# Neighbourhood attention's scores with all 128 array rows, band and context in one matmul

## The chip, the cores and the metric

One core of a Trainium2 chip runs the kernel. The metric is device microseconds of one execution; the number compared is the median of several runs. Engines are named TensorE (PE in the profile, PEld its weight loads), VectorE (DVE), ScalarE (ACT), GpSimd (POOL) and SyncE (SP, which issues the transfers).

## What is computed

Two layers of a trunk over 512 latent tokens and 256 context tokens of width 1024. Each layer norms its input, projects it, runs three attention branches (retention, neighbourhood attention, grouped-query attention), gates and merges them. The change concerns neighbourhood attention: 8 heads of 64, each latent query against a band of nearby keys and all 256 context keys, with one softmax over both.

```python
def neighbourhood_attention(q, k, v, kc, vc, rpb, rows):
...
        s = jnp.einsum('brjqhd,brwjkhd->bhrjqwk', qb, kb).astype(jnp.float32) * scale + bias[None]
        s = jnp.where(col_ok[:, :, None, :], s, -jnp.inf)
        s_ctx = jnp.einsum('brjqhd,blhd->bhrjql', qb, kc).astype(jnp.float32) * scale
        s_all = jnp.concatenate([s.reshape(s.shape[:5] + (n_loc,)), s_ctx], axis=-1)
        p = jax.nn.softmax(s_all, axis=-1)
...
        return jnp.einsum('bhrjqwk,brwjkhd->brjqhd', p_loc, vb) + jnp.einsum('bhrjql,blhd->brjqhd', p_ctx, vc)
```

In the first layer the context tokens are queries too: 256 of them attend to the 256 context keys of their head.

## The kernel before

Numbers are carried as two float32r parts, an upper one and the rest, so a product is a sum of matmuls: upper by upper, upper by lower, lower by upper. A projection adds three matmuls for each of 8 feature tiles (L278 to L280: `hxh`, `hxl` are the input's parts, `whi`, `wlo` the weight's) over 512 latent and then 256 context columns. Weights are streamed: SyncE loads `raw`, ScalarE makes `whi` (L262), GpSimd (at times VectorE) makes `wlo` (L264).

In neighbourhood attention one feature tile `p` (0 to 3) holds two heads `e`. For a head, Q (`q`) stands with its upper part in the 64 rows of the head and its lower part in the other 64. `K1` has K's upper part in both halves, so one matmul of 128 rows gives (Q upper + Q lower) by K upper (L588). Q upper by K lower is a second matmul with the 64 rows of the head alone (L589); `K2`, one tile for both heads, has the lower part of head 0 in rows 0 to 63, that of head 1 in rows 64 to 127. In the profile both `K1` and `K2` are called `k`, in the program's order `k1` and `k2`.

A score step `s_step(j)` does this for 128 queries: two matmuls for the band (256 columns from 64 * BAND0[j]), two for the context (256 columns from NX = 512), into one PSUM bank `s` of 512 columns, of which there are two. VectorE adds the bias and takes the maximum (L591), then come the negated maximum (L598), the exponentials on ScalarE (L600), the reciprocal (L602) and the scaling on VectorE or GpSimd (L605). Transposes (L617), their split into parts (L438, L439) and the products with V (L628, L629) follow. The context queries' scores of the first layer go through `smm` (L638, L639), 256 columns a matmul.

TensorE's order is written by hand: `window` lays attention steps and projection matmuls into one stream, by weights and nominal costs that are fixed numbers (0.45 us for a score step). Tile 0 of a layer begins with eight score steps; later the second head's scores go between the first head's transposes and products, and the next tile's between the second's. The other engines' order comes from a scheduler with priorities. `NA.open` takes the memory of the branch, once a layer.

Of the kernel before, what the change touches and what calls it, by code (L numbers as in the profile page):

```python
# [39 lines left out]
def trunk_kernel(ctx: ExitStack, tc: tile.TileContext, xt, wcol, wv, adaw, wbr, wout, nabias, vecs,  # L40
# [26 lines left out]

    # ---------------------------------------------------------------- order of the tensor engine's work
    clock = [0.0]
# [5 lines left out]
    def defer(us, fn):  # L75
        """emit fn once the tensor engine has been given us more microseconds of work"""
        waiting.append([clock[0] + us, len(waiting), fn])
# [69 lines left out]

    # ---------------------------------------------------------------- constants
    npool_cm = pool("nm0")
# [13 lines left out]
    def block_ones(t, blocks):  # L163
        """ones within blocks of partitions, zeros between them"""
        nc.vector.tensor_scalar(t, ident, 0.0, float(len(blocks) == 1), op0=ALU.mult, op1=ALU.add)
        if len(blocks) > 1:
            for a, b in blocks:
                nc.vector.tensor_scalar(t[a:b, a:b], ident[a:b, a:b], 0.0, 1.0, op0=ALU.mult, op1=ALU.add)
        return t
# [30 lines left out]

    # ---------------------------------------------------------------- helpers
    def rsqrt(dst, ss, n, mul, eps):
# [10 lines left out]
    def rsqrt_wide(r, x, t, ss, mul, eps):  # L213
        """r = 1 / sqrt(ss * mul + eps), whole rows of tokens; x and t are scratch"""
        nc.vector.tensor_scalar(x, ss, mul, eps, op0=ALU.mult, op1=ALU.add)
        nc.vector.tensor_scalar(r.bitcast(I32), x.bitcast(I32), -0.5, float(0x5F3759DF), op0=ALU.mult, op1=ALU.add)
        for _ in range(3):
            nc.scalar.activation(t, r, AF.Square)  # L218
            nc.vector.scalar_tensor_tensor(t, t, -0.5, x, op0=ALU.mult, op1=ALU.mult)  # L219
            nc.vector.scalar_tensor_tensor(r, t, 1.5, r, op0=ALU.add, op1=ALU.mult)  # L220

    def col_sums(m, sh, sl, n, tag):
        """sums over the partitions that m groups, on every partition"""
        ss = bank(tag)
        mm(ss[:, :n], lhsT=m, rhs=sh, start=True, stop=False)
        mm(ss[:, :n], lhsT=m, rhs=sl, start=False, stop=True)
        return ss[:, :n]
# [102 lines left out]

    # ---------------------------------------------------------------- modulation
    def ada_load(l, s, apool, bufs):
# [4 lines left out]
    def ada_slice(l, s, apool, bufs, raw=None):  # L337
        """slice s < 8: shift and scale of feature tile s; 8..11: gates of two feature tiles"""
        if raw is None:
# [26 lines left out]

    # ---------------------------------------------------------------- norms
    def sumsq(acc, x, first, c, npool, bufs=2):
# [37 lines left out]

    # ---------------------------------------------------------------- pieces of attention
    def gate_evac(sg):
# [15 lines left out]
    def split_rows(hi, lo, rl, r0, src, scale, cols):  # L424
        rows = slice(r0, r0 + 64)
        nc.scalar.activation(hi[rows, cols], src[rows], AF.Copy, scale=scale)
        nc.vector.scalar_tensor_tensor(lo[rl:rl + 64, cols], src[rows], scale, f(hi[rows, cols]),
                                       op0=ALU.mult, op1=ALU.subtract)
# [13 lines left out]
    def ctx_steps(st, smm, scale, vs, get_ot, r0, ap, bufs):  # L442
        """softmax(s) @ v of the 256 context queries: score, transpose and product steps"""
        def sx():
# [35 lines left out]
        return (0.7, 0.45, sx), (1.0, 0.45, tx), (1.0, 0.45, pvx)  # L480

    def pv_(P, j):
        t, pad = P[j]
        return t[:, :, pad:pad + 256]

    # ---------------------------------------------------------------- neighbourhood attention
    class NA:
# [6 lines left out]
        def open(self):  # L494
            env["gcm"] = pool(f"gp{self.l}")
            env["gp"] = env["gcm"].__enter__()
            self.cm = pool(f"na{self.l}")
            self.ap = self.cm.__enter__()

        def open_work(self):  # L500
# [17 lines left out]
        def u_k(self, p):  # L518
            def ev(ps, o, n):
                if o == 0:  # L520
                    self.K1[p] = [self.ap.tile([128, NT], F32R, tag="k1", name="k1", bufs=4) for _ in range(2)]
                    self.K2[p] = self.ap.tile([128, NT], F32R, tag="k2", name="k2", bufs=2)
                c = slice(o, o + n)
                K1, K2 = self.K1[p], self.K2[p]
                split_rows(K1[0], K2, 0, 0, ps, 1.0, c)
                split_rows(K1[1], K2, 64, 64, ps, 1.0, c)
                nc.vector.tensor_copy(K1[0][64:128, c], f(K1[0][0:64, c]))
                nc.vector.tensor_copy(K1[1][0:64, c], f(K1[1][64:128, c]))
            return u_proj(ap_wcol[self.l][CT_NK + p], G_ALL, ev)
# [28 lines left out]
        def heads(self, p):  # L558
            """score, transpose, product and context steps of the two heads of feature tile p"""
            ap, l = self.wp, self.l  # L560
            heads = []
            for e in range(2):
                r0 = 64 * e
                rr = slice(r0, r0 + 64)
                st = {}
# [12 lines left out]

                def s_step(j, e=e, st=st, rr=rr, start=start):
                    Q, K1, K2 = self.Q[p], self.K1[p], self.K2[p]  # L580
# [4 lines left out]
                    qc = slice(128 * j, 128 * j + 128)  # L585
                    for o, kc in ((0, 64 * BAND0[j]), (256, NX)):
                        kk = slice(kc, kc + 256)
                        mm(s[:, o:o + 256], lhsT=Q[e][:, qc], rhs=K1[e][:, kk], start=True, stop=False)  # L588
                        mm(s[:, o:o + 256], lhsT=Q[e][rr, qc], rhs=K2[rr, kk], start=False, stop=True)  # L589
                    v = BVAR[j]  # L590
# [41 lines left out]

                def smm(s, e=e, rr=rr):
                    Q, K1, K2 = self.Q[p], self.K1[p], self.K2[p]
                    for i in range(2):
                        qc = slice(NX + 128 * i, NX + 128 * i + 128)
                        o = s[:, 256 * i:256 * i + 256]
                        mm(o, lhsT=Q[e][:, qc], rhs=K1[e][:, NX:NT], start=True, stop=False)  # L638
                        mm(o, lhsT=Q[e][rr, qc], rhs=K2[rr, NX:NT], start=False, stop=True)  # L639
                S = [(0.7, 0.45, lambda j=j, s_step=s_step: s_step(j)) for j in range(4)]  # L640
# [7 lines left out]
        def steps(self, p, need):  # L648
            """the second head's scores go beside the first head's products, and the next tile's first head's
            scores (once the projections in need are through) beside the second's"""  # L650
            if p == 0:
# [21 lines left out]

    # ---------------------------------------------------------------- grouped-query attention
    class GQA:
# [26 lines left out]
        def stats_evac(self, t, w, ntok, done, lag):  # L702
            """t = raw * w; sums of squares by token and head, then done(sums)"""
            st = {}
# [208 lines left out]

    # ---------------------------------------------------------------- retention
    class RET:
# [152 lines left out]

    # ---------------------------------------------------------------- merges
    def u_merge(l, b, d, g, m, getpool):  # L1070
# [34 lines left out]

    # ---------------------------------------------------------------- the plan
    plan = []
# [3 lines left out]
    def start_phase(na, first):  # L1111
        """the input norm; the first projections advance feature tile by feature tile"""
        acc = npool.tile([128, NT], F32, name="acc")
# [113 lines left out]

    # weights in the order of use
    def add(us):
# [16 lines left out]
    def finish(l, m, mtp):  # L1246
# [53 lines left out]
        def norm_part(o, n, use, go, w1=3.0, w2=4.0):  # L1300
            """go(wait, fn): run fn, after wait microseconds of other work"""
            r = cp.tile([128, 6], F32, tag="rstd", name="rstd", bufs=2)

            def one():
                ss = stat_mm(accs["t"], o, n)
                nb = n // 128
                rsqrt(r[:, o // 128:o // 128 + nb], ss[:, :nb], nb, 1.0 / D, EPS)
                go(w2, two)

            def two():  # L1310
                bc = bcast_mm(r, o, n)
                for k in range(KT):
                    use(k, bc[:, :n], o, n)
            go(w1, one)
# [48 lines left out]

# [1 line left out]
def _perm():  # L1365
# [111 lines left out]
```

## Time and profile before

| | |
|---|---|
| median of 3 runs | 1785.39 us (1783.95 to 1786.2) |
| span of the profiled execution, first to last instruction | 1782.7 us |
| TensorE busy | 1714.5 us (96%) |
| VectorE busy | 1055.3 us (59%) |
| ScalarE busy | 797.9 us (45%) |
| GpSimd busy | 550.8 us (31%) |
| granted clock of TensorE, mean | 0.995 of full speed |

The span and the runs are 2.7 us apart. The first layer's neighbourhood attention lies at 75.5 to 272 us of the span, the second's at 1058.9 to 1222; the stages with grouped-query attention between about 290 and 560 and between 1240 and 1440. A matmul's row is longer than the time until the next one starts, since matmuls are pipelined: rates are read from the starts of neighbouring rows, not from the durations.

### The profile page before, as it was taken

What the parts mean: (1) busy time and instruction counts of PE and PEld (TensorE: products, weight loads), DVE (VectorE), ACT (ScalarE), POOL (GpSimd) and SP (SyncE); (2) the same over time, 40 slices, a digit from 0 to 9 for tenths busy, and PEclk for the clock granted to TensorE, in tenths of its full rate; (3) what the DMA queues carried; (4) which work ended last, traced back from release to release, by engine and by line L of the source; (5) the groups of instructions that cost most, each with busy time, mean ns of one, the idle gap of its engine ahead of it and who ended that gap; (6) DMA issues with size and microseconds to landing.
All of it is one profiled execution on the core that took longest, in us unless ns stands there. A gap on an engine that the chain in (4) does not pass through costs nothing. (4 is left out here: it accounts for less than half of the span.)

```text
span 1782.7 us, 26397 instructions
## 1 busy us (share of the span) xinstructions
PE 1714.5 (96%) x10068; PEld 1458.9 (82%) x10068; DVE 1055.3 (59%) x2201; ACT 797.9 (45%) x1570; POOL 550.8 (31%) x478
## 2 busy tenths in 40 slices
PE   6999999999999999999999999999999999999997
PEld 4777878888999888888887888777788897887786
DVE  7566467657654565565324755567876645545446
ACT  4355454555553443443223434555555544444342
POOL 1233222333233222222222322332433333333442
PEclk9999999999999999999999999999999999999999
DMA  7211102111111211113536521211111122221245
GB/s 310 74 54 44 55 24 65 43 48 36 48 37 53 65 48 48 60 48 139 217 130 209 170 86 42 78 45 60 60 48 60 48 74 69 69 68 63 90 131 170
DMA packets 43054, 146.40 MB, mean 82 GB/s; under 512 B 4912, under 2 KB 10160, under 8 KB 39856
## 3 DMA queue, kind: packets, MB, share of 16 engines
q1 hardware_dynamic: 42928, 144.72, 24.2%
q8 instruction: 79, 1.29, 0.3%
q14 instruction: 47, 0.39, 0.1%
HBM read 140.51 MB, written 4.19 MB: 81 GB/s over the span
## 5 line engine op out<-in xcount | busy, mean ns | idle before, releaser
L264 POOL TENSOR_TENSOR wlo<-raw,whi 128x512 fp32r<-128x512 f32 x345 | 456.9, 1330 | 975.5 <-ACT whi L262 927.2
L278 PE MATMUL pj<-hxh,whi 128*128 128x512 f32 (+1 forms) x1448 | 531.9, 367 | 10.6 <-DVE ql L967 3.9
L279 PE MATMUL pj<-hxl,whi 128*128 128x512 f32 (+1 forms) x1448 | 509.7, 352 | 0.8 <-DVE hxl L404 0.8
L280 PE MATMUL pj<-hxh,wlo 128*128 128x512 f32 (+1 forms) x1448 | 509.3, 352 | 0.0
L262 ACT CAST whi<-raw 128x512 fp32r<-128x512 f32 x376 | 231.3, 618 | 302.3 <-PE pj L279 220.4
L278 PEld LDWEIGHTS pj<-hxh,whi 128*128 128x128 f32 x1448 | 273.9, 189 | 48.0 <-DVE ql L967 5.8
L280 PEld LDWEIGHTS pj<-hxh,wlo 128*128 128x128 f32 x1448 | 273.6, 189 | 38.9
L279 PEld LDWEIGHTS pj<-hxl,whi 128*128 128x128 f32 x1448 | 274.6, 190 | 26.3 <-DVE hxl L404 1.9
L439 DVE TENSOR_TENSOR pl<-pt,ph 128x512 fp32r<-128x512 f32 (+2 forms) x208 | 127.1, 626 | 63.0 <-ACT ph L438 60.8
L438 ACT CAST ph<-pt 128x512 fp32r<-128x512 f32 (+2 forms) x208 | 108.0, 534 | 91.4 <-PE pt L617 49.5
L278 PE MATMUL pj<-gat,whi 128*128 128x512 f32 (+1 forms) x416 | 144.4, 347 | 2.6 <-ACT gat L910 2.0
L279 PE MATMUL pj<-gat,whi 128*128 128x512 f32 (+1 forms) x416 | 142.4, 342 | 0.5 <-DVE gat L1264 0.3
L280 PE MATMUL pj<-gat,wlo 128*128 128x512 f32 (+1 forms) x416 | 142.1, 342 | 0.0
L310 PE MATMUL pj<-whi,hxh 128*128 128x256 f32 x384 | 111.0, 289 | 1.4 <-DVE kl L967 0.8
L312 PE MATMUL pj<-whi,hxl 128*128 128x256 f32 x384 | 109.3, 285 | 0.0
L311 PE MATMUL pj<-wlo,hxh 128*128 128x256 f32 x384 | 109.3, 285 | 0.0
L278 PEld LDWEIGHTS pj<-gat,whi 128*128 128x128 f32 x416 | 78.8, 189 | 11.9 <-ACT gat L910 2.5
L280 PEld LDWEIGHTS pj<-gat,wlo 128*128 128x128 f32 x416 | 78.8, 190 | 9.3
L855 ACT ACTIVATE p<-p,nm,rq 128x768 f32<-128x768 f32 x64 | 65.4, 1023 | 46.9 <-DVE nm L853 46.4
L279 PEld LDWEIGHTS pj<-gat,whi 128*128 128x128 f32 x416 | 79.0, 190 | 8.9 <-DVE gat L911 0.5
L846 DVE TENSOR_SCALAR_CACHE_REDUCE p<-s 128x384 f32<-128x384 f32 x128 | 69.0, 554 | 26.9 <-PE s L845 25.5
L1099 DVE SCALAR_TENSOR_TENSOR mt<-mt,pj 128x512 f32<-128x512 f32 (+1 forms) x48 | 28.6, 596 | 91.8 <-PE pj L280 91.2
(264 smaller groups left out, 3012.1 us busy)
## 6 DMA issues: line engine op xcount, KB each, us to landing
raw<-in_wcol_dram SPq DMA_DIRECT2D x116, 512.0 KB, 3.5
araw<-in_adaw_dram SPq DMA_DIRECT2D x24, 1024.0 KB, 6.5
raw<-in_wout_dram SPq DMA_DIRECT2D x32, 512.0 KB, 3.5
raw<-in_wbr_dram SPq DMA_DIRECT2D x24, 512.0 KB, 3.5
raw<-in_wv_dram SPq DMA_DIRECT2D x16, 512.0 KB, 3.5
bias<-in_nabias_dram SPq DMA_DIRECT2D x16, 384.0 KB, 3.0
x<-in_xt_dram SPq DMA_DIRECT2D x8, 384.0 KB, 5.7
xo<-in_xt_dram SPq DMA_DIRECT2D x8, 256.0 KB, 3.8
```

The source lines that it names most:

```text
L262: nc.scalar.copy(hi, raw[:, c])
L264: lo_eng.tensor_tensor(lo, raw[:, c], f(hi), op=ALU.subtract)
L278: mm(ps, lhsT=sh, rhs=mh, start=start, stop=False)
L279: mm(ps, lhsT=sh, rhs=ml, start=False, stop=False)
L280: mm(ps, lhsT=sl, rhs=mh, start=False, stop=stop)
L310: mm(o, lhsT=sh[:, tok], rhs=hi, start=(k == 0), stop=False)
L311: mm(o, lhsT=sh[:, tok], rhs=lo, start=False, stop=False)
L312: mm(o, lhsT=sl[:, tok], rhs=hi, start=False, stop=(k == KT - 1))
L438: nc.scalar.copy(ph[:, :n], pt[:, :n])
L439: nc.vector.tensor_tensor(pl[:, :n], pt[:, :n], f(ph[:, :n]), op=ALU.subtract)
L846: nc.vector.tensor_scalar(P[:, jj, kk], s[:, :384], 1.0, -3.0e38, op0=ALU.mult, op1=ALU.max, accum_out=mx[:, i:i + 1])
L855: nc.scalar.activation(P[:, a], P[:, a], AF.Exp, bias=nm[:, a:a + 1], scale=rqe[:, 2 * hf + a:2 * hf + a + 1], accum_out=sm[:, a:a + 1])
```

## The change

K's lower part gets a tile of 128 rows for each head, with zeros in the 64 rows that are not the head's. There are two pairs of such tiles, taken in turn by the feature tiles, as `k2` had two buffers. GpSimd fills the zeros once a layer, when the branch's memory is opened. The second score matmul then uses all 128 rows of Q and of the tile; the lower part of Q meets the zeros. With both operands of full height, band and context go into one matmul of 512 columns, whose moving operand is an access pattern of two blocks of 256 columns, 512 - 64 * BAND0[j] apart (`two_blocks`; for j = 3 the blocks touch). The context queries' scores keep their 256 columns and get the full-height tile. The program also gives its dynamic transfers a smaller scratch. Comments and docstrings that fell away are not shown.

```diff
+    def two_blocks(t, a, b, n):
+
+        v = t[:, a:a + n]
+        return bass.AP(v.tensor, v.offset, [list(v.ap[0]), [b - a, 2], [1, n]])
...
             self.cm = pool(f"na{self.l}")
             self.ap = self.cm.__enter__()
+            self.kz = [[self.ap.tile([128, NT], F32R, name=f"kz{i}{e}") for e in range(2)] for i in range(2)]
+            for pair in self.kz:
+                for e, t in enumerate(pair):
+                    nc.gpsimd.memset(f(t[64 - 64 * e:128 - 64 * e, :]), 0.0)
...
-                    self.K2[p] = self.ap.tile([128, NT], F32R, tag="k2", name="k2", bufs=2)
+                    self.K2[p] = self.kz[p % 2]
...
-                split_rows(K1[0], K2, 0, 0, ps, 1.0, c)
-                split_rows(K1[1], K2, 64, 64, ps, 1.0, c)
+                split_rows(K1[0], K2[0], 0, 0, ps, 1.0, c)
+                split_rows(K1[1], K2[1], 64, 64, ps, 1.0, c)
...
-                    for o, kc in ((0, 64 * BAND0[j]), (256, NX)):
-                        kk = slice(kc, kc + 256)
-                        mm(s[:, o:o + 256], lhsT=Q[e][:, qc], rhs=K1[e][:, kk], start=True, stop=False)
-                        mm(s[:, o:o + 256], lhsT=Q[e][rr, qc], rhs=K2[rr, kk], start=False, stop=True)
+                    kc = 64 * BAND0[j]
+                    mm(s, lhsT=Q[e][:, qc], rhs=two_blocks(K1[e], kc, NX, 256), start=True, stop=False)
+                    mm(s, lhsT=Q[e][:, qc], rhs=two_blocks(K2[e], kc, NX, 256), start=False, stop=True)
...
                         mm(o, lhsT=Q[e][:, qc], rhs=K1[e][:, NX:NT], start=True, stop=False)
-                        mm(o, lhsT=Q[e][rr, qc], rhs=K2[rr, NX:NT], start=False, stop=True)
+                        mm(o, lhsT=Q[e][:, qc], rhs=K2[e][:, NX:NT], start=False, stop=True)
...
-    nc = _bacc.Bacc("TRN2", target_bir_lowering=False, num_devices=1)
+    nc = _bacc.Bacc("TRN2", target_bir_lowering=False, num_devices=1, dynamic_dma_scratch_size=1024)
```

On TensorE the first two score steps of the first layer and the projection behind them read as follows before the change (`s` is the scores' bank, `pj` a projection's):

```order
L588 MATMUL s_805<-k1_579,q_569 128x256
L589 MATMUL s_805<-k2_581,q_569 128x256
L588 MATMUL s_805<-k1_579,q_569 128x256
L589 MATMUL s_805<-k2_581,q_569 128x256
L588 MATMUL s_811<-k1_579,q_569 128x256
L589 MATMUL s_811<-k2_581,q_569 128x256
L588 MATMUL s_811<-k1_579,q_569 128x256
L589 MATMUL s_811<-k2_581,q_569 128x256
L278 MATMUL pj_785<-hxh_171,whi_606 128x512
L279 MATMUL pj_785<-hxl_172,whi_606 128x512
```

Eight matmuls of 256 columns stand ahead of the projection. The same place on TensorE after the change, where L595 and L596 are the two lines of the score step and `kz00` the new tile of head 0:

```order
L595 MATMUL s_812<-k1_587,q_577 128x512
L596 MATMUL s_812<-kz00_566,q_577 128x512
L595 MATMUL s_816<-k1_587,q_577 128x512
L596 MATMUL s_816<-kz00_566,q_577 128x512
L278 MATMUL pj_792<-hxh_171,whi_613 128x512
L279 MATMUL pj_792<-hxl_172,whi_613 128x512
```

Four of 512 columns are left, and nothing else has moved between them and the projection. On GpSimd the start of the first layer before the change reads (`bias` and `pb` are fills for the first two heads):

```order
L264 TENSOR_TENSOR wlo<-raw,whi 128x512 x7
L570 MEMSET bias 128x256
L573 MEMSET pb 128x4x64
L570 MEMSET bias 128x256
L573 MEMSET pb 128x4x64
L264 TENSOR_TENSOR wlo<-raw,whi 128x512 x6
```

The four fills there stand between the seventh and the eighth weight split. The same place on GpSimd after the change, with the zero fills at L507:

```order
L264 TENSOR_TENSOR wlo<-raw,whi 128x512 x7
L507 MEMSET kz_566 64x768
L507 MEMSET kz_567 64x768
L507 MEMSET kz_568 64x768
L264 TENSOR_TENSOR wlo<-raw,whi 128x512
L507 MEMSET kz_569 64x768
L264 TENSOR_TENSOR wlo<-raw,whi 128x512
L578 MEMSET bias 128x256
L581 MEMSET pb 128x4x64
L578 MEMSET bias 128x256
L581 MEMSET pb 128x4x64
L264 TENSOR_TENSOR wlo<-raw,whi 128x512 x4
```

Three zero fills stand ahead of the eighth split, the fourth ahead of the ninth, and the older fills behind it. In the second layer two stand ahead of each of the last two splits before the same place.

## Rows read from the trace of the kernel before

**Rows 1.** Page, part 1: engine, busy us (share of the span), instructions.

```profile
PE 1714.5 (96%) x10068; PEld 1458.9 (82%) x10068; DVE 1055.3 (59%) x2201; ACT 797.9 (45%) x1570; POOL 550.8 (31%) x478
```

**Rows 2.** Stretches: us, busy (count) of PE, PEld, DVE, ACT, POOL; clock, DMA share, GB/s.

```profile
75.50:272.00 196.50, 194.07 (x1089) 155.65 (x1088) 114.03 (x257) 98.35 (x234) 57.73 (x70) 1.00 0.16 50
75.70:89.90 14.20, 14.20 (x54) 9.00 (x53) 7.50 (x25) 5.42 (x14) 3.42 (x6) 1.00 0.29 95
290.00:560.00 270.00, 266.98 (x1691) 239.81 (x1690) 174.69 (x439) 143.14 (x291) 86.12 (x76) 1.00 0.15 45
1058.90:1222.00 163.10, 160.15 (x846) 126.06 (x845) 93.61 (x220) 80.28 (x178) 50.06 (x52) 1.00 0.18 58
1058.90:1073.00 14.10, 14.10 (x52) 8.64 (x50) 6.57 (x22) 6.30 (x15) 4.68 (x5) 1.00 0.24 81
1240.00:1440.00 200.00, 190.56 (x1033) 159.60 (x1032) 143.17 (x370) 110.79 (x212) 74.85 (x58) 1.00 0.18 58
```

**Rows 3.** TensorE's timeline, one score step: start, us, line, out<-in, rows*columns of weights, shapes.

```profile
113.94 0.28 PE L588 MATMUL s<-k,q 128*128 128x256 f32 x1
114.15 0.39 PE L589 MATMUL s<-k,q 64*128 64x256 f32 x1
114.47 0.38 PE L588 MATMUL s<-k,q 128*128 128x256 f32 x1
114.78 0.38 PE L589 MATMUL s<-k,q 64*128 64x256 f32 x1
115.09 0.50 PE L278 MATMUL pj<-hxh,whi 128*128 128x512 f32 x1
115.43 0.39 PE L279 MATMUL pj<-hxl,whi 128*128 128x512 f32 x1
```

**Rows 4.** TensorE's timeline, projections of 256 and 512 columns.

```profile
110.26 0.28 PE L280 MATMUL pj<-hxh,wlo 128*128 128x256 f32 x1
110.38 0.40 PE L278 MATMUL pj<-hxh,whi 128*128 128x512 f32 x1
```

**Rows 5.** Weight loads of the score step in rows 3; idle time before, releaser.

```profile
114.15 0.18 PEld L589 LDWEIGHTS s<-k,q 64*128 64x128 f32 x1 [0.25 <-issue]
```

**Rows 6.** TensorE's timeline, four score matmuls of grouped-query attention, two projections.

```profile
314.78 0.33 PE L844 MATMUL s<-gk,q 128*128 128x384 f32 x1
314.95 0.34 PE L845 MATMUL s<-gk,q 128*128 128x384 f32 x1
315.13 0.34 PE L844 MATMUL s<-gk,q 128*128 128x384 f32 x1
315.31 0.35 PE L845 MATMUL s<-gk,q 128*128 128x384 f32 x1
315.49 0.40 PE L278 MATMUL pj<-hxh,whi 128*128 128x512 f32 x1
315.72 0.40 PE L279 MATMUL pj<-hxl,whi 128*128 128x512 f32 x1
```

**Rows 7.** Lines L589 and L639: count, ns min/median/max, first and last start.

```profile
L589 PE MATMUL s<-k,q x128: 377/381/385, 75.9 to 1203.2; 64*128 64x256 f32 x128
L639 PE MATMUL s<-k,q x16: 377/381/382, 97.2 to 261.4; 64*128 64x256 f32 x16
```

**Rows 8.** TensorE's timeline, first matmul of a context step and the projection behind.

```profile
96.97 0.28 PE L638 MATMUL s<-k,q 128*128 128x256 f32 x1
...
98.12 0.50 PE L278 MATMUL pj<-hxh,whi 128*128 128x512 f32 x1
```

**Rows 9.** ScalarE's timeline, one exponential in the first layer's start.

```profile
79.60 0.72 ACT L600 ACTIVATE pa<-pa,nm 128x512 f32<-128x512 f32 x1 [1.42 <-DVE nm L598]
```

**Rows 10.** GpSimd's timeline, a fill and two weight splits; idle time before, releaser.

```profile
50.36 0.31 POOL L570 MEMSET bias<- 128x256 f32 x1
...
55.53 1.30 POOL L264 TENSOR_TENSOR wlo<-raw,whi 128x512 fp32r<-128x512 f32 x1 [2.72 <-ACT whi L262]
...
1028.15 1.27 POOL L264 TENSOR_TENSOR wlo<-raw,whi 128x512 fp32r<-128x512 f32 x1 [4.11 <-ACT whi L262]
```

More of the change, by code (lines that the diff above doesn't have):

```diff
@@ L563, in heads @@
                 r0 = 64 * e
-                rr = slice(r0, r0 + 64)
                 st = {}
@@ L577, in start, with s_step @@
                         st[nm] = ap.tile([128, 4], F32, tag=nm, name=nm, bufs=2)
-                def s_step(j, e=e, st=st, rr=rr, start=start):
+                def s_step(j, e=e, st=st, start=start):
                     Q, K1, K2 = self.Q[p], self.K1[p], self.K2[p]
@@ L631, in pv_step, with smm @@
                         pv_out(st["ops"], NX, self.get_ot(p), r0, 0)
-                def smm(s, e=e, rr=rr):
+                def smm(s, e=e):
                     Q, K1, K2 = self.Q[p], self.K1[p], self.K2[p]
```

## The prediction

> **What bounds the kernel now.** I read the page's busy times first. TensorE is busy for 1714.5 us, 96% of a span of 1782.7 us [rows 1]. A busy TensorE may still be stalled inside its busy time, so I went on to the two stretches of neighbourhood attention. In the first layer TensorE is idle for 196.50 - 194.07 = 2.4 us of 196.5, in the second for 163.10 - 160.15 = 3.0 us of 163.1 [rows 2]. Nothing that other engines do is on the path there: whatever shortens TensorE's own stream shortens the run, until somebody else is late.
>
> Then the stream itself, by the starts of neighbouring rows. One score step is four matmuls of 256 columns [rows 3]. The reader should see the steps between starts: 0.21, 0.32, 0.31, 0.31 us, so 1.15 us from the first score matmul to the projection behind it, and then 0.34 us until the next projection. An undisturbed 256-column matmul takes 0.12 us between starts [rows 4] and an undisturbed projection of 512 columns 0.23 us (the last two of [rows 6]). So four matmuls that should take 0.48 us take 1.15, and they delay the one behind them by another 0.10. Every second matmul of the step has 64 rows of weights, the others 128. The weight load of the first 64-row matmul stands idle for 0.25 us with "issue" as the releaser, that is, with no semaphore behind it [rows 5]. The grouped-query attention is the counterexample in the same trace: four score matmuls of 384 columns, all with 128 rows, go at 0.17, 0.18, 0.18 and 0.18 us, 0.71 us for half as many columns again, and the projection behind them loses nothing [rows 6]. So the stall sits at each change between 128 and 64 rows, not in the columns.
>
> **The change part by part.** (1) Score steps. There are 128 of the 64-row score matmuls, two to a step, so 64 steps [rows 7]. A step becomes two matmuls of 512 columns with 128 rows. Their price is the projection's 0.23 us each [rows 6], also what the grouped-query rows give per column (0.178 x 512 / 384 = 0.237). So 0.46 us instead of 1.15 + 0.10: 0.79 us less for each, 64 x 0.79 = 50.6 us.
>
> (2) Context steps of the first layer: 16 of the 64-row matmuls, two to a step, 8 steps [rows 7]. One takes 1.15 us now [rows 8] plus the 0.10; afterwards it is four 256-column matmuls of 128 rows, 4 x 0.12 = 0.48. 8 x 0.77 = 6.2 us.
>
> Both lie wholly on the path: 56.8 us. What no row shows is a moving operand of two separate blocks, since every one in these rows is contiguous. I price it like a contiguous one, because the same columns are streamed; a better price than 0.23 us has no row, and a worse one is a rival below. The order of instructions on VectorE, ScalarE and SyncE stays as it was but for rows that change places at three points, and on TensorE the score rows alone differ, so no other wait is added there.
>
> [...]
>
> (3) What comes back as waits. TensorE now runs ahead faster than VectorE and ScalarE were used to. The hard place is the start of each layer's stretch: eight score steps with only a few projections between them. In 14.2 us (first layer) VectorE is busy 7.5 us, and in 14.1 us (second) 6.6 us [rows 2]. TensorE's need there falls by 8 x 0.79 = 6.3 us to 7.9 and 7.8 us. VectorE has to read each score bank before its buffer (there are two) is used again, and its queue holds, behind those reads, reciprocals that wait for ScalarE's exponentials, 0.72 us each and two to a pair [rows 9]. If everything fits, 0 comes back. If VectorE has to sit through two such pairs of about 1.8 us (with their accumulator reads), the stage takes 7.5 + 3.6 = 11.1 us and 3.2 us come back. I take 2.0 for each, since VectorE's need of 6.6 to 7.5 us is close to the 7.9 before any stop for ScalarE.
>
> For the rest of the stretches the nearest rows are the grouped-query stages, which already run full-height scores. There TensorE is idle 3.0 us of 270.0 (1.1%) with VectorE 65% busy, and 9.4 of 200.0 (4.7%) with 72% [rows 2]. After the change the two stretches of together 360 us last some 303, with VectorE at (114.0 + 93.6) / 303 = 69%. In between, about 3%, or 9 us, against 5.4 us now: +3.6 with the starts included. At 1.1% it would be 3.3 us, no increase; at 4.7%, 14.2, an increase of 9. I take +5 in all (two starts at 2.0 and 1.0 elsewhere); the ends are 0 and 9 + 2 x 3.2 = 15.
>
> (4) The zero fills: four per layer, 64 x 768, on GpSimd. The nearest row is 0.31 us for 128 x 256 [rows 10], so 0.93 us each and 3.7 us a layer. In the first layer three take the place of the bias fills from 50.36 us on and are through at about 53.2; the weight split behind them starts at 55.53 today, because it waits for ScalarE's upper part [rows 10]. The fourth pushes the next split back by 0.9 us and the bias fills behind that, which nobody reads before the stretch at 75.7 [rows 2]. In the second layer GpSimd is idle for 4.11 us at the place [rows 10], and one split starts up to 1.9 us later, behind two fills; its reader is the last part of a token projection which has not begun. So the idle time hides them; that cover gone, the second would cost at most the 1.9. Both places lie in a norm, where VectorE and ScalarE are waited for while GpSimd fills, so I allow 2 us either way and take +0.5.
>
> Sum: 56.8 - 5 - 0.5 = 51.3 us. The span falls from 1782.7 to about 1731.4. The median of the runs, 1785.39, is 2.7 us above the span; with the same margin it comes to **1734 us**.
>
> **The rivals.** *VectorE and ScalarE become the bound of the stretches.* The waits then take half of the gain instead of a tenth: for it speaks that VectorE's share rises to 69% in the mean and near 95% at the starts; against it that the grouped-query stage bears 72% with 4.7% of waits. Priced at twice the upper end of (3), 30 us come back: 56.8 - 30 = 27, about 1758 us.
>
> *Full-height loads are exposed in the new step.* Each of the 128 + 32 matmuls then adds its load of 0.19 us, 30 us in all, to what it takes; 1785.4 - 51.3 + 30, about 1764 us. For it nothing in these rows; against it the grouped-query rows [rows 6].
>
> *The two-block operand streams slowly*, and this is the one that ends slower than before. One step in four has its blocks side by side (256 and 512), so 48 steps or 96 matmuls have a gap. At half pace each costs 0.23 us more: 22 us back, 1756 us. It decides from 51.3 / 96 = 0.53 us more per matmul, that is 0.76 us for one; at a quarter of the pace (0.92 us) it is 96 x 0.69 = 66 us more, and the kernel ends at 1800 us. No row speaks for it or, with such an operand, against it; the column pace elsewhere is the same for 256, 384 and 512.
>
> **How the numbers follow.** The forecast 86 in 100; VectorE as bound 7; exposed loads 2; a two-block operand at half pace 3, at quarter pace or worse 2. The forecast's own range is its bounds: waits of 0 to 15 us and the fills of -2 to +2, so a gain of 40 to 59 us, 1726 to 1746. I widen the top a little to 1747; the other cases lie outside, and they and a miss of my bounds hold under 2 in 10. A change below 0.2% (3.6 us) could not be told from none. Faster by more than that is 0.97, within it 0.01, slower 0.02.
>
> **What would show it.** In the new trace the two score matmuls of a step should be 0.23 us apart and the projection behind the second 0.23 us later and again 0.23 to its neighbour: then (1) holds. If they are 0.42 apart with the load idle before them, the loads are exposed; 0.46 or more with no load waiting is the two-block read. The step of the context rows should be 0.12 us. The stretches should last about 163 and 135 us; new rows of TensorE waiting for VectorE at the score line or at the transposes, above all in the first 10 us of each, are the price of (3), and more than 15 us of them would make the forecast wrong. The zero fills should take about 0.9 us and no projection should wait for a weight split behind them.

## The result and the profile after

The changed kernel takes 1743.92 us (median of four runs, 1739.51 to 1745.52) against 1784.69 us (1783.95 to 1786.2). The ratio is 0.9764, 95% interval 0.9753 to 0.9776: 40.8 us less, where 51.3 was forecast. The profiled execution has a span of 1742.2 us, 40.5 us less than before, at a mean granted clock of 0.993 (0.995 before).

The first part of the page after, busy us and share of each engine:

```profile
PE 1665.9 (96%) x9940; PEld 1439.5 (83%) x9940; DVE 1056.7 (61%) x2201; ACT 796.8 (46%) x1570; POOL 556.4 (32%) x486
```

TensorE has 128 matmuls fewer and is still busy 96% of the time [rows 1]; GpSimd has the eight fills more. VectorE and ScalarE do what they did, in 40 us less.

The groups of the changed kernel, shapes kept apart: count, busy us, mean ns, idle time before and its releaser:

```profile
L595 PE MATMUL s<-k,q 128*128 128x512 f32 x64 | 26.5, 415 | 2.3 <-DVE k L536 1.9
L596 PE MATMUL s<-kz,q 128*128 128x512 f32 x64 | 25.2, 393 | 0.0
L507 POOL MEMSET kz<- 64x768 f32 x8 | 5.9, 734 | 0.4
```

The second score matmul of a step (against `kz`, the low part in its zero-padded tile) never waits. A fill takes 0.73 us.

TensorE's timeline after, a context step and a score step, each with its neighbour (start, us):

```profile
103.43 0.28 PE L645 MATMUL s<-k,q 128*128 128x256 f32 x1
103.55 0.28 PE L646 MATMUL s<-kz,q 128*128 128x256 f32 x1
...
103.79 0.28 PE L646 MATMUL s<-kz,q 128*128 128x256 f32 x1
103.91 0.28 PE L278 MATMUL pj<-hxh,whi 128*128 128x256 f32 x1
...
112.74 0.40 PE L595 MATMUL s<-k,q 128*128 128x512 f32 x1
112.98 0.39 PE L596 MATMUL s<-kz,q 128*128 128x512 f32 x1
113.20 0.34 PE L635 MATMUL pv<-ph,v 128*128 128x384 f32 x1
113.38 0.34 PE L636 MATMUL pv<-pl,v 128*128 128x384 f32 x1
```

The score step takes 0.24 + 0.22 = 0.46 us where it took 1.15 and held up its neighbour by 0.10 [rows 3]; what stands behind it starts at its own pace. The context step takes four times 0.12 us [rows 8]. These are the forecast's figures to the hundredth, and the other steps read alike where no wait stands in them. So the 56.7 us of TensorE's own time are gone; 16.2 of them came back as something else.

**Where they came back.** Apart from the score rows, TensorE runs the same instructions in the same order in both kernels, so the two traces can be laid side by side at fixed rows. Good ones are the first score matmul of each layer and the four matmuls at L225 that follow the stretches (two behind each). Line L225 before, and L225 and L595 after: count, ns, first and last start:

```profile
L225 PE MATMUL pt<-ks,blk x4: 277/337/396, 278.7 to 1228.0; 128*128 128x512 f32 x2, 128*128 128x256 f32 x2
```

```profile
L225 PE MATMUL pt<-ks,blk x4: 277/337/396, 257.4 to 1185.4; 128*128 128x512 f32 x2, 128*128 128x256 f32 x2
...
L595 PE MATMUL s<-k,q x64: 387/396/504, 77.5 to 1159.9; 128*128 128x512 f32 x64
```

The second layer's first score matmul starts at 1038.13 us after and at 1058.92 before [rows 2]. From these marks, in us:

| piece | before | after | gain | of this expected from the steps | back |
|---|---|---|---|---|---|
| start to the first score | 75.7 | 77.5 | -1.8 | 0 | 1.8 |
| first layer, score to L225 | 203.0 | 179.9 | 23.1 | 31.4 | 8.3 |
| L225 to the second layer's first score | 780.2 | 780.7 | -0.5 | 0 | 0.5 |
| second layer, score to the last L225 | 169.1 | 147.3 | 21.8 | 25.3 | 3.5 |
| last L225 to the end | 554.7 | 556.8 | -2.1 | 0 | 2.1 |

So 11.8 us came back inside the two stretches, 1.8 ahead of the first, 2.1 at the end. No piece without score steps gained time, so the smaller scratch for transfers, the other difference between the kernels, brought nothing that shows.

The rows' starts tell where in the stretches. Of the 8.3 us of the first, 2.9 stand at the second product of probabilities and V (L636), 2.1 at the transposes of the context queries' probabilities (L469), 0.7 at the first product (L635) and 2.2 at score steps. Of the 3.5 us of the second, 2.3 stand at score steps.

The two stretches after, columns as in [rows 2]:

```profile
77.40:250.70 173.30, 165.25 (x1025) 143.32 (x1024) 115.25 (x256) 97.62 (x234) 57.77 (x70) 1.00 0.18 58
1036.40:1179.50 143.10, 138.37 (x792) 117.04 (x791) 95.36 (x223) 80.33 (x179) 50.80 (x53) 1.00 0.22 69
```

TensorE's idle time rises from 2.4 and 3.0 us to 8.05 and 4.73, by 7.4 us together; VectorE is busy 67% of either. Whom TensorE waits for in the first and in the second stretch (us, times, longest):

```profile
PE pv L636 <- DVE pl L439: 4.7, 6, 1.0
PE pt L469 <- POOL pc L461: 1.5, 2, 0.8
PE pv L635 <- ACT ph L438: 0.7, 1, 0.7
...
PE pv L636 <- DVE pl L439: 1.9, 5, 0.5
PE s L595 <- DVE k L536: 1.8, 2, 1.1
```

L636 is the second probability-times-value product; it reads `pl`, the low part of the transposed probabilities, which VectorE computes at L439. L469 waits for GpSimd's scaling of the context queries' probabilities (L461). In the kernel before, the wait for `pl` in the first stretch was:

```profile
PE pv L629 <- DVE pl L439: 1.3, 4, 0.5
```

In the second stretch it was 1.7 us, so there it is not new. One of the waits after, on TensorE and then on VectorE and GpSimd:

```profile
106.45 0.39 PE L635 MATMUL pv<-ph,v 128*128 128x512 f32 x1
107.69 0.50 PE L636 MATMUL pv<-pl,v 128*128 128x512 f32 x1 [0.86 <-DVE pl L439]
```

```profile
104.16 1.37 DVE L537 CAST k<-k 64x512 fp32r<-64x512 f32 x1
...
106.96 0.68 DVE L439 TENSOR_TENSOR pl<-pt,ph 128x512 fp32r<-128x512 f32 x1
```

```profile
103.96 1.29 POOL L264 TENSOR_TENSOR wlo<-raw,whi 128x512 fp32r<-128x512 f32 x1 [5.90 <-ACT whi L262]
```

The product starts 1.24 us after its predecessor, which at column pace would be 0.23. On VectorE the split stood behind a copy of K's upper part into the other half of its tile (L537), with three shorter instructions between them and no idle time. That copy took 1.37 us, beside a weight split of 1.29 us on GpSimd; a copy of the same shape at 61.97 us, where GpSimd has nothing to do, takes 0.42 us. The slow copy ends 0.28 us behind GpSimd's split (105.53 and 105.25 us).

The slow copy itself is not new. In the kernel before it stands at the same place and takes as long:

```profile
108.01 1.37 DVE L528 CAST k<-k 64x512 fp32r<-64x512 f32 x1
```

There the product came 0.47 us after its predecessor (111.07 and 111.54 us). TensorE comes earlier now, and VectorE does not.

**The fills.** A copy of this kind is worse off ahead of the first stretch. GpSimd, VectorE and TensorE there, after:

```profile
55.64 1.30 POOL L264 TENSOR_TENSOR wlo<-raw,whi 128x512 fp32r<-128x512 f32 x1 [2.87 <-ACT whi L262]
56.87 0.74 POOL L507 MEMSET kz<- 64x768 f32 x1
57.57 1.29 POOL L264 TENSOR_TENSOR wlo<-raw,whi 128x512 fp32r<-128x512 f32 x1
58.80 0.31 POOL L578 MEMSET bias<- 128x256 f32 x1
...
59.55 0.31 POOL L581 MEMSET pb<- 128x256 f32 x1
```

```profile
57.02 3.13 DVE L536 CAST k<-k 64x512 fp32r<-64x512 f32 x1
```

```profile
63.86 0.36 PE L310 MATMUL pj<-whi,hxh 128*128 128x256 f32 x1 [2.34 <-DVE kz L427]
```

The fourth zero fill and, behind the next split, the four fills of `bias` and `pb` now stand right beside VectorE's copy. GpSimd works without a gap from 55.64 to 59.86 us, and the copy ends only at 60.15: 3.13 us. Before, it took:

```profile
56.95 1.42 DVE L527 CAST k<-k 64x512 fp32r<-64x512 f32 x1
```

VectorE's splits of K come 1.7 us later, and TensorE waits 2.34 us for a bank, against 0.62 us at the same matmul before.

### The profile page after: what moved, and what is told of

Read it like the earlier page. It is cut to its first block, busy times and chain, and to the rows that moved or that the text cites. A ratio compares the mean times of both kernels' runs of the same rounds, so it can differ in the third digit from the quotient of the medians.

```text
span 1742.2 us, 26141 instructions
## 1 busy us (share of the span) xinstructions
PE 1665.9 (96%) x9940; PEld 1439.5 (83%) x9940; DVE 1056.7 (61%) x2201; ACT 796.8 (46%) x1570; POOL 556.4 (32%) x486
## 3 DMA queue, kind: packets, MB, share of 16 engines
q8 instruction: 78, 1.28, 0.3%
## 5 line engine op out<-in xcount | busy, mean ns | idle before, releaser
L439 DVE TENSOR_TENSOR pl<-pt,ph 128x512 fp32r<-128x512 f32 (+2 forms) x208 | 126.7, 625 | 52.9 <-ACT ph L438 50.7
```

Of the source, the lines that this page charges most:

```text
L439: nc.vector.tensor_tensor(pl[:, :n], pt[:, :n], f(ph[:, :n]), op=ALU.subtract)
```

## Experiments

All ratios are against the kernel before, run on the same chip.

**Full height alone.** The padded tiles, but four matmuls of 256 columns as before:

```diff
-mm(s, lhsT=Q[e][:, qc], rhs=two_blocks(K1[e], kc, NX, 256), ...)
-mm(s, lhsT=Q[e][:, qc], rhs=two_blocks(K2[e], kc, NX, 256), ...)
+for o, kc in ((0, 64 * BAND0[j]), (256, NX)):
+    kk = slice(kc, kc + 256)
+    mm(s[:, o:o + 256], lhsT=Q[e][:, qc], rhs=K1[e][:, kk], ...)
+    mm(s[:, o:o + 256], lhsT=Q[e][:, qc], rhs=K2[e][:, kk], ...)
```

> Half of the change alone: the zero-padded full-height tiles, but band and context still in two matmuls of 256 columns each, four to a step. Theory (the stall sits at each change between 128 and 64 rows): no change of height is left, the four matmuls stand 0.12 us apart, 0.48 us a step against 0.46 in the changed kernel, so 64 x 0.02 = 1.3 us more than that kernel: about 1745 us, nearly the whole gain. Rival (the gain comes from the wider matmul): the steps stay at 0.3 us a matmul and the time is near 1780 us.

Measured: 1742.63 us (1741.55 to 1744.73), ratio 0.9757 [0.974, 0.9773]. Its score step on TensorE:

```profile
113.39 0.28 PE L596 MATMUL s<-k,q 128*128 128x256 f32 x1
113.51 0.28 PE L597 MATMUL s<-kz,q 128*128 128x256 f32 x1
...
113.75 0.29 PE L597 MATMUL s<-kz,q 128*128 128x256 f32 x1
113.88 0.34 PE L636 MATMUL pv<-ph,v 128*128 128x384 f32 x1
```

0.49 us for the step. The height alone brings the whole gain, as was expected. The merged matmul adds nothing that can be measured in the time, and the operand of two blocks costs nothing either (0.46 us a step with it).

**Merging alone.** Two matmuls of 512 columns, the low part still with 64 rows:

```diff
+mm(s, lhsT=Q[e][:, qc], rhs=two_blocks(K1[e], kc, NX, 256), ...)
+mm(s, lhsT=Q[e][rr, qc], rhs=two_blocks(K2[rr], kc, NX, 256), ...)
```

> The other half alone: one 512-column matmul over two blocks for the upper part and one for the lower, the lower still with the 64 rows of its head. Theory: one change of height in and one out are left of four in a step; by the starts in the kernel before a change costs 0.09 to 0.19 us and the way out another 0.10, so a step takes 0.84 to 0.94 us (with the 0.10) instead of 1.25: 64 x 0.31 to 0.41 = 20 to 26 us less than before, 1759 to 1765 us with no new waits, some 3 us more with them. Context steps stay as before. Rival (width carries the gain): near 1745 us.

Measured: 1766.55 us (1765.3 to 1767.61), ratio 0.9889 [0.9873, 0.9905]. TensorE's matmuls, then its weight loads:

```profile
115.00 0.40 PE L591 MATMUL s<-k,q 128*128 128x512 f32 x1
115.33 0.50 PE L592 MATMUL s<-k,q 64*128 64x512 f32 x1
115.76 0.44 PE L631 MATMUL pv<-ph,v 128*128 128x384 f32 x1
```

```profile
115.33 0.18 PEld L592 LDWEIGHTS s<-k,q 64*128 64x128 f32 x1 [0.36 <-issue]
115.76 0.19 PEld L631 LDWEIGHTS pv<-ph,v 128*128 128x128 f32 x1 [0.25 <-issue]
```

The step takes 0.33 + 0.43 = 0.76 us, and the next matmul starts 0.28 us after the one at 115.76 instead of 0.18. With two changes of height instead of four it keeps about half of the stall, and half of the gain is missing, as was expected. Both loads at a change, 128 to 64 rows and back, stand idle with no semaphore behind them, for 0.36 and 0.25 us. The two changes cost 0.40 us more than full height would, 0.10 of it behind the step, so 0.2 us for each; the four of the step before cost 0.78, nearly the same for each.

One thing these runs leave open. Every 64-row matmul in them stands between 128-row ones, and halving the changes also halved the 64-row matmuls. Whether a 64-row matmul behind another of 64 rows would stall as well, no run shows.

**The fills once, at the kernel's beginning.** The four tiles are kept for both layers and filled in the first microseconds; the fills in `NA.open` go:

```diff
+kz_all = [[cp.tile([128, NT], F32R, name=f"kz{i}{e}") for e in range(2)] for i in range(2)]
+for pair in kz_all:
+    for e, t in enumerate(pair):
+        nc.gpsimd.memset(f(t[64 - 64 * e:128 - 64 * e, :]), 0.0)
```

> The changed kernel with the zero tiles kept for both layers and filled once, at the start, where GpSimd has nothing to do. Theory (the fills lengthen GpSimd's run of work at 56.9 to 59.9 us, and a VectorE copy that has to stand behind it takes 3.13 us, so TensorE waits 2.34 us): the copy at 57 us takes 1.5 us or less, that wait goes, the score steps begin 1.8 us earlier, at about 75.7 us, and the time is about 2 us lower than the changed kernel's at the same clock. Rival (the tiles or their place in memory are what delays): the start stays at 77.5 us.

Measured: 1742.28 us (1741.18 to 1747.02), ratio 0.9759 [0.9738, 0.9779]. In the time this can't be told from the changed kernel; the 2 us that were expected don't show. The trace of it is clear on the mechanism; VectorE's copy, then TensorE's waits from 54 to 66 us:

```profile
57.46 1.42 DVE L537 CAST k<-k 64x512 fp32r<-64x512 f32 x1
```

```profile
PE pj L314 <- DVE kz L431: 0.6, 1, 0.6
```

Without fills on GpSimd the copy takes its old 1.42 us and TensorE waits 0.6 us again. The first score matmul starts at 76.2 us, 1.3 earlier than in the changed kernel (75.7 was expected).

**The copies on ScalarE.** If VectorE's copies, slow beside GpSimd, hold up the splits that TensorE waits for, moving them off VectorE should give some of the waits back:

```diff
-nc.vector.tensor_copy(K1[0][64:128, c], f(K1[0][0:64, c]))
-nc.vector.tensor_copy(K1[1][0:64, c], f(K1[1][64:128, c]))
+nc.scalar.copy(K1[0][64:128, c], f(K1[0][0:64, c]))
+nc.scalar.copy(K1[1][0:64, c], f(K1[1][64:128, c]))
```

> The changed kernel with the copies of K's upper part into the other half of its tile on ScalarE instead of VectorE: 4 copies of 0.3 to 1.4 us for each of 8 feature tiles leave VectorE, some 12 to 15 us, and ScalarE gets as much. Theory (after the change TensorE waits for VectorE in the two stretches, about 8 us in the first layer and 3.5 in the second): these waits fall by a third to a half and the 3.13 us copy beside GpSimd goes, so 4 to 6 us lower than the changed kernel. Rival (ScalarE is late as well, it makes the upper part that VectorE waits for): same or slower, with TensorE waiting for ScalarE in place of VectorE.

Measured: 1735.3 us (1734.76 to 1735.97), ratio 0.9716 [0.9698, 0.9734]. This is the best version, faster than both kernels, and in the medians by more than was expected. TensorE's waits in the first stretch, and the marks at L225 and L595:

```profile
PE pv L636 <- DVE pl L439: 1.9, 4, 1.0
PE pt L469 <- POOL pc L461: 1.5, 2, 0.8
```

```profile
L225 PE MATMUL pt<-ks,blk x4: 277/336/396, 251.1 to 1177.5; 128*128 128x512 f32 x2, 128*128 128x256 f32 x2
...
L595 PE MATMUL s<-k,q x64: 389/397/504, 74.8 to 1152.0; 128*128 128x512 f32 x64
```

By the marks of the table above, against the changed kernel: the first score starts 2.7 us earlier; the first stretch is 3.6 shorter (176.3), the second 1.3 (146.0, from 1031.5 us); 0.3 lies between, and the end is 1.4 shorter. The product's wait for `pl` falls from 4.7 to 1.9 us in the first stretch, while the one for GpSimd's scaling stays. So moving the copies takes 4.9 us out of the stretches. Not all of the difference in the medians is theirs: part is the granted clock (last section). At an equal clock of 0.996 the changed kernel had runs of 1739.5 and, repeated, 1741.5 us, and this one 1734.8 and 1735.1: 4.4 to 6.7 us, about the 4 to 6 that were expected.

**The same move in the kernel before.** Is that a gain that was there all along, or one that the change made?

> The kernel before with the same copies of K's upper part on ScalarE, and nothing else changed. In the changed kernel this move gave some 8 us. Theory (the shorter score steps brought VectorE onto the path; before, TensorE's stalls covered it): here it gives 0 to 3 us, the 0.6 us wait at the start of the first layer and a few waits at the products, so 1783 to 1786 us. Rival (VectorE's copies were on the path all along): some 8 us less than before, about 1777 us.

Measured: 1783.72 us (ten runs, 1781.41 to 1785.28), ratio 0.9989 [0.998, 0.9999]: 1.9 us between the medians, against 8 to 9 behind the change. The granted clock differs here too. At 0.995 two runs of this version took 1781.6 and 1782.6 us and seven of the kernel before 1783.5 to 1785.7, so some 3 us at an equal clock, against 4.4 to 6.7. The marks at L225:

```profile
L225 PE MATMUL pt<-ks,blk x4: 277/337/396, 277.1 to 1226.2; 128*128 128x512 f32 x2, 128*128 128x256 f32 x2
```

With the first score matmuls at 75.2 and 1058.2 us, the gain is 0.6 us ahead of the first stretch, 1.0 in it and 1.1 in the second. Behind the change the same pieces gave 2.7, 3.6 and 1.3. So the copies cost some 2.7 us on TensorE's path before and 7.6 after. The change put more of them on the path, ahead of the first stretch and in it; in the second layer they cost what they had cost. Of the 11.8 us that came back in the stretches, 4.9 - 2.1 = 2.8 are then put down to the copies.

**Both moves together** (fills at the beginning, copies on ScalarE).

> Both at once: zero tiles filled at the start and the copies on ScalarE. Theory (the fills cost time only because a VectorE copy stood behind GpSimd): with the copies gone from VectorE the place of the fills no longer matters, so the time is that of the kernel with the copies alone, 1735 us within 1 us, and the score steps begin at the same time within 0.5 us. Rival (the fills delay something else as well, a weight split say): about 1.5 us lower again.

Measured: 1736.33 us (1734.4 to 1737.6), ratio 0.9728 [0.9713, 0.9742]. With the copies off VectorE, the place of the fills brings no gain that shows: the first score starts at 75.5 us here and at 74.8 with the fills in their place, and 0.5 of these 0.7 us lie ahead of TensorE's first matmul (14.3 and 13.8 us). That is a little outside the 1735 us within 1 and the 0.5 us that were expected, and on the side away from the rival. So the fills cost time through VectorE's copy beside them, not through GpSimd's own queue.

**The changed kernel again**, on a second chip, beside the last two.

> The changed kernel itself, unaltered, beside the other two on one chip. Theory (stretches at half clock, of 3.4 or 6.8 us each, fall differently from run to run): 1739 to 1746 us, lower times going with a higher mean granted clock (0.996 against 0.992), about 4 us between the two. Rival (the spread has nothing to do with the clock): no such order.

Measured: 1744.38 us (1741.45 to 1745.92), ratio 0.9772 [0.9757, 0.9786], the same as the first time. Sorted by the granted clock its runs are 1741.5 (0.996), 1744.2 (0.993), 1744.5 and 1745.9 (both 0.992).

## Why the prediction was right, and where its sum was off

The time lies in the range of 1726 to 1747 us, in the likeliest case, but 10 us above the value. The mechanism on TensorE was right. The range held with 3 us to spare: its bounds allowed 17 us to come back, and 16.2 did, 2.6 of them in pieces that the sum did not list (between the layers and at the end). By the forecast's own steps:

- **(1) and (2), the steps.** Right: 0.46 us for a score step and 0.48 for a context step. That the change of height and not the columns makes the stall was the reading of [rows 3, 5, 6], and the two halves of the change, run apart, show it: the height alone gives everything.
- **(3), the waits.** The term that was mis-sized: 11.8 us came back where 5 were taken (the bounds, 0 and 15, held). The place was wrong too. Of the 5 us, 4 were put on the starts. There TensorE goes from the first score to the projection behind the eighth step in 6.82 us in the first layer and 7.88 in the second, against 12.70 and 14.07 before: gains of 5.9 and 6.2 of the 6.2 us that the steps give up to that matmul, so the starts lose some 0.4 us together. The "1.0 elsewhere" is what failed: about 11 us. It was scaled from the grouped-query stages' idle shares with VectorE's mean load, and a mean load says little here. What counted was who stood ahead, in its engine's queue, of the result that TensorE needed next. K's copies ahead of the split `pl` are one case that was tested, worth 2.8 us. The other 9 us come back with the copies on ScalarE as well: 2.1 at the transposes that wait for GpSimd's scaling, the rest in small pieces at products and score steps, and what would remove them was not tested. 7.4 us of the 11.8 show as more idle time of TensorE in the stretches; the rest is lost in delays such as the 1.24 us above, of which the trace calls only 0.86 idle.
- **The stretches' lengths.** 163 and 135 us were given as a sign, but they don't follow from the steps: 196.5 - 31.4 is 165.1 and 163.1 - 25.3 is 137.8, before any wait. Measured: 173.3 and 143.1.
- **(4), the fills.** 1.8 us against 0.5, inside the 2 us allowed, by another way than the one that was weighed. The forecast looked at what stands behind the fills on GpSimd, and there indeed nobody waited. Its 2 us were for VectorE's part of a norm; what ran beside the fills was a copy of K. A fill was 0.73 us, not 0.93.
- **The end.** 2.1 us back in a part that the change doesn't touch were not in the sum. They go with the granted clock: it stands at 0.50 near 1241 and 1716 us of this profile, where the profile before has no such stretch, and the version with the copies moved, at 0.996, needs 555.4 us there, this profile at 0.993 needs 556.8.
- **The margin** between span and run was 1.8 us in this execution, 2.7 in the forecast: 0.9 us the other way.

The rivals: *exposed loads* fell: a load of 128 rows lasts 0.19 us, but the second score matmul starts 0.24 us after the first and never waits. *The two-block operand* streams like a contiguous one, 0.24 and 0.22 us a matmul against the projection's 0.23 [rows 6]. *VectorE as the bound* went in the right direction, with VectorE 67% busy, but 12 us came back and not 30. ScalarE had room: it took the 32 copies at 0.40 to 0.62 us each, and nothing that shows was lost by it.

## What to carry to other kernels

Where 64-row matmuls alternated with 128-row ones, each change cost about 0.2 us, so padding the short operand with zeros to full height was worth 40 us here without any merging, though it multiplies by zeros. After such a gain on the engine that bounds, look for work that used to be covered: here it was copies on the engine that TensorE waits for next, worth some 3 us to move before the change and 4.4 to 6.7 after it, at an equal clock. Where a fill or a split is added on GpSimd, look at what VectorE does beside it (here a copy that took 1.42 us came to 3.13), not only at what follows on GpSimd's own queue.

## What the hardware showed beyond what was expected

**A VectorE copy beside several GpSimd instructions took 3.13 us.** That is a copy that takes 0.42 where GpSimd has nothing to do; it ran beside splits and fills without a gap and ended 0.29 us behind the last of them (60.15 and 59.86 us). The run with full height alone shows 3.15 at the same place. The fills only write, and still the copy lasted through them. But a copy need not last until GpSimd stops. In the same trace another copy of this shape was done while two splits ran without a gap (VectorE's row, then GpSimd's):

```profile
1143.14 0.99 DVE L537 CAST k<-k 64x512 fp32r<-64x512 f32 x1
```

```profile
1142.57 2.71 POOL L264 TENSOR_TENSOR wlo<-raw,whi 128x512 fp32r<-128x512 f32 x2 [9.71 <-ACT whi L262]
```

It ended at 1144.13 us, 0.28 behind the first split's end at 1143.85, and the second split took 1.44 us where the first took 1.28. What decides whether a copy ends before GpSimd stops stays open; no run was made for it.

**The same wait, with and without a loss of clock.** The stretch from 63 to 68 us holds TensorE's wait of 2.3 us in the changed kernel's first profile and in its second (columns as in [rows 2]):

```profile
63.00:68.00 5.00, 4.14 (x35) 4.17 (x36) 1.72 (x5) 0.99 (x3) 0.00 (x0) 1.00 0.02 5
...
1239.00:1244.00 5.00, 4.02 (x14) 3.65 (x15) 3.76 (x16) 2.65 (x5) 1.29 (x1) 0.66 0.00 0
```

```profile
63.00:68.00 5.00, 4.01 (x22) 4.04 (x23) 1.85 (x5) 1.12 (x3) 0.00 (x0) 0.66 0.02 5
```

In the first profile the granted clock stays at 1.00 and 35 matmuls fit; in the second it is 0.66 in the mean, matmuls of 256 columns start 0.21 us apart until 66.9 us and 0.12 from 67.1 us on, and 22 fit. 13 matmuls at 0.12 us are 1.6 us, for the same wait of 2.33 or 2.34 us. The stretch at 1239 us shows a lower clock in the first profile too, 0.50 from 1240.0 to 1243.3 us, behind a wait of 2.06 us. Whether a wait of about 2 us is followed by a lower clock differs between executions of one kernel, and the runs of the changed kernel spread over 6 us, in the order of their clocks of 0.992 to 0.996. Removing a wait of that length may thus bring more than the wait itself, and the medians of the copies' move would fit that. It is not shown: with fills and copies both moved the runs still had 0.993 to 0.995. What decides it in a given execution stays open.
